# An encoder trunk on one core: the bias of group D in a query tile, the latents of group A through DRAM as one part

## The chip, the core and the metric

The kernel runs on one core of a Trainium2 chip. Such a core has five engines that run their own instruction streams in order: TensorE (PE, with its weight loads shown as PEld), VectorE (DVE), ScalarE (ACT), GpSimd (POOL) and SyncE (SP), which here issues nearly all transfers between DRAM and the on-chip memory SBUF. Matrix products land in PSUM, eight banks of 128 x 512 float32. The metric is the device time in microseconds of one execution. Three runs of the kernel before took 2723.59 to 2733.64 us, with a median of 2730.46.

## The reference

Two layers over 1024 tokens of width 1024, all in float32. Each layer: RMSNorm, one input projection, four groups of attention heads side by side, one output projection, then an MLP with squared ReLU. The groups, cut to what matters here:

```python
cq, ckv, kr, bq, bk, bv, ck.., dq, dk, dv = split(rms_norm(x, norm1_g) @ w_in)
# A (4 heads): queries, keys and values come from two small "latents"
q = rms_norm(cq, q_norm_g) @ w_uq          # cq: 192 wide, q_norm_g a gain per column
c = rms_norm(ckv, kv_norm_g)               # ckv: 128 wide
k, v = c @ w_uk, c @ w_uv
# B: differential attention, normed per head; dense like A
# C: each block of 128 queries sees 3 blocks of keys, with a mask
# D: neighbourhood on a 64-wide grid: scores + relative-position bias, softmax, values
mix = concat([rms_norm(y_a, g_a), y_b, rms_norm(y_c, g_c), rms_norm(y_d, g_d)])
x = x + mix @ w_out
```

## The kernel before

Every float32 product is made of three passes: operands are split into a high part (ACT copies it to the PE's format) and a low part (the rest, by DVE or POOL), and a product adds high x high, low x high and high x low (`passes`, L220 to L222). Operands lie transposed, columns on the 128 partitions, in tiles of 128 x 1024 or 128 x 512.

A layer's attention is woven from two streams (`weave`): one "main" stream of attention steps and one "fill" stream of projections. In order: the fused projections of B, then B's attention (`attn_b`) with the latents' projections (`proj_latent`) and D's projections as fill; then D's attention (`attn_d`) with C's projections and the latents' way up to A's queries, keys and values (`latent_up`) as fill; then C (`attn_c`) and A (`attn_a`) with the first half of the output projection as fill. A scheduler turns this into one fixed order of instructions for each engine, by priorities and by when buffers come free; only the MLP's PE order is written out by hand. Loads and stores all go to SP's queue in that order; the scheduler gives eight completion counters to them in turn, so that a transfer is not issued before the eighth before it has landed.

What the change and the prediction touch:

- Projected queries, keys and values are written to DRAM as two parts (`emit_parts`, `to_parts`, `to_values`) and loaded per head into tiles of the pool `xp` with the tag "x" (`stack`, eight of them for all groups): four per head in B and A, three per head in D (`qs`, two `ks`), four per pair of heads in C.
- The latents: `proj_latent` makes `cq` (128 + 64 rows) and `ckv` (128). `latent_parts` squares them for the norm, splits them with their gain into the two parts `both` (ACT L197, DVE L198) and stores these in `lat`, shape 2 x 3 x 128 x 1024. `latent_up` loads both parts into six tiles `latp` of the pool `big` (the 64-row one twice, into both halves of the partitions) and multiplies them (L220 to L222, and L720 for the 64-row one).
- `attn_d` loads a bias of 128 x 6 x 128 per head into one buffer "bias"; the mask of `attn_c` is loaded into the same buffer after it.
- `banded` makes a head of C or D: `score` (L977, then DVE's minimum with the bias or mask, L1053 or L1084, then the exponential on ACT), `parts` (transposes L986 and their split), `apply` (value sums, L998 and L999). The value sums of keys 0 to 4 go to the first half of the queries, then those of keys 3 to 7 to the second half. Each half starts with a matmul of zeros (`zeroed`, L1027) into the one bank "pv"; `pv_out` reads it out (ACT L746, DVE L188). PSUM is shared out as mm=2, tr=2, sb=3, pv=1; "mm" takes the products of the fill stream and small sums and transposes.
- `rstd_cols` sums squares over the partitions and makes reciprocal roots; `rows_of` turns its columns into rows in DRAM (`drows`), and `spread` loads such rows over the partitions (`rz`, `rq`, `rkv`). `sub_norm`, the norm of B per head, has two sums per column (g=2).

Of the kernel before, what the change touches and what calls it, by code (L numbers as in the profile page):

```python
# [13 lines left out]
F = mybir.dt.float32  # L14
R = mybir.dt.float32r
# [5 lines left out]
P = 128  # L21
S = 1024
# [6 lines left out]
T_CQ, T_CQR, T_CKV = 0, 1, 2  # L29
# [69 lines left out]
def layout(i):  # L99

    def padded(a, axis):

        z = np.zeros([1 if n == axis else s for n, s in enumerate(a.shape)], a.dtype)
        return np.concatenate([a, z], axis)

    n = LAYERS
    out = host_constants()
    out["x"] = i["x"][0].T.reshape(8, P, S)
    out["w_in"] = tiles_of(padded(i["w_in"], 2)[:, :, np.concatenate(input_tiles())], 4)

    wo = i["w_out"].reshape(n, 8, P, DM)[:, [2, 3, 6, 7, 4, 5, 0, 1]].reshape(n, DM, DM)
    out["w_out"] = tiles_of(wo, 4)
    out["w_up"] = tiles_of(i["w_up"], 4)
    out["w_down"] = tiles_of(i["w_down"], 4)

    uq = i["mla_w_uq"].reshape(n, 192, 4, 96)
    cols = [uq[..., 64:96].reshape(n, 192, 4, 2, 16).transpose(0, 1, 3, 2, 4).reshape(n, 192, P)]
    cols += [uq[:, :, 2 * t:2 * t + 2, 0:64].reshape(n, 192, P) for t in range(2)]
    q = np.stack(cols, 1)

    q = np.concatenate([q, q[:, :, 128:192]], 2).reshape(n, 6, P, P)
    kv = [i[w][:, None, :, t * P:(t + 1) * P] for w in ("mla_w_uk", "mla_w_uv") for t in range(2)]
    w = np.concatenate([q] + kv + [np.zeros((n, 2, P, P), uq.dtype)], 1)
    out["w_lat"] = w.reshape(n, 3, 4, P, P).transpose(0, 1, 3, 2, 4)
    rpb = padded(i["na_rpb"].reshape(n, 4, 465), 2)
    rpb[..., 465] = NEG
    out["bias"] = rpb[..., neighbours()]
    col = lambda a: a.reshape(n, -1, P).transpose(2, 0, 1).reshape(P, -1)
    gq = np.concatenate([i["mla_q_norm_g"], np.zeros((n, 64), np.float32)], 1)
    sub = np.concatenate([i["diff_subln_g"]] * 2, 1)  # L130
    lam = np.stack([i["diff_lambda_" + s] for s in ("q1", "q2", "k1", "k2")], 1)
    wide = lambda a: np.broadcast_to(a.reshape(1, -1), (P, a.size))
    out["par"] = np.concatenate(
        [col(i["norm1_g"]), col(i["norm2_g"]), i["final_norm_g"].reshape(8, P).T]
        + [col(i["out_g_" + s]) for s in ("mla", "swa", "na")]
        + [col(i["mla_kv_norm_g"]), col(gq), col(sub), wide(i["swa_sinks"])], 1)
    out["lam"] = wide(lam)
    return {k: np.ascontiguousarray(v) for k, v in out.items()}
# [7 lines left out]
class Trunk:  # L146
# [107 lines left out]
    def rstd_cols(self, sq, count, rhs, tag="mm"):  # L254

        nc = self.nc
        g = rhs.shape[1]
        n = sq.shape[1] // P
        ps = self.bank(tag, [P, n * g])
        for t in range(n):  # L260
            nc.tensor.matmul(ps[:, t * g:(t + 1) * g], sq[:, t * P:(t + 1) * P], rhs, start=True, stop=True)
        ms = self.cp.tile([P, n * g], F, tag="ms", name="ms")
        nc.vector.tensor_scalar(ms, ps, 1.0 / count, EPS, ALU.mult, ALU.add)
        return self.rsqrt_cols(ms)
# [15 lines left out]

    def spread(self, dst, rows, j=0, g=1):

        src = rows.rearrange("(t g) p -> g t p", g=g)[j]
        n = dst.shape[0]
        self.load(dst.rearrange("p (t q) -> p t q", t=8), src.partition_broadcast(n))

    def spread_here(self, dst, col):

# [88 lines left out]
    def attention(self, l):  # L377
        nc, tc, d = self.nc, self.tc, self.d
        rb = self.rb
        sbuf = lambda name, side="left": tc.tile_pool(name=f"{name}{l}", bufs=1, reuse_waits="tile", side=side)  # L380
        w_in = lambda t: d["w_in"][l, t]
        dr = lambda shape, name: self.dram.tile(shape, F, tag=name, bufs=1, name=name)
# [3 lines left out]
        qb, kb, vb = dr([2, 2, 4, 16, 2, S], "qb"), dr([2, 2, 4, 16, 2, S], "kb"), dr([4, P, 8, P], "vb")  # L386
        qd, kd, vd = dr([2, 2, P, S], "qd"), dr([2, 2, P, S], "kd"), dr([4, P, 8, P], "vd")
        qc, kc, vc = dr([2, 2, 2, 32, 2, S], "qc"), dr([2, 2, 32, 2, S], "kc"), dr([2, P, 8, P], "vc")
        lat, krd = dr([2, 3, P, S], "lat"), dr([2, 16, 2, S], "krd")
        qa = dr([2, 2, P, S], "qan"), dr([2, 4, 16, 2, S], "qar")  # L390
        ka, va = dr([2, 2, P, S], "kan"), dr([4, P, 8, P], "va")

# [25 lines left out]
        rows = []  # L418
        y = {"b": [], "d": [], "c": [], "a": []}
        with ExitStack() as stack, ExitStack() as att:  # L420
            self.ap = att.enter_context(sbuf("att"))
            with self.banks(mm=2, tr=2, sb=3, pv=1):
                with sbuf("proj", "right") as self.pp:
# [8 lines left out]
                    xs = self.normed(self.g1[:, l], lambda n: self.big_tile(R, n))  # L432
# [57 lines left out]
            with self.banks(mm=8):  # L490
# [12 lines left out]
                for m in range(self.EARLY, 8):  # L503
# [4 lines left out]
                    for n in range(2):  # L508
# [3 lines left out]
                        ps = self.mm_ps()  # L512
# [131 lines left out]
            self.keep(dst[:, :, n * 4:n * 4 + 4].rearrange("h p k e -> p h (k e)"), b.bitcast(F))  # L644
        return then

    def latent_parts(self, y, g, rows, n, dst, squares):

        nc = self.nc
        sl = slice(n * 512, n * 512 + 512)  # L650
        sq = self.part()
        nc.scalar.activation(sq[:rows], y[:rows], AF.Square)
        ps = self.bank("mm", [P, 4])
        for t in range(4):
            nc.tensor.matmul(ps[:, t:t + 1], sq[:rows, t * P:(t + 1) * P], self.ones[:rows, 0:1],
                             start=True, stop=True)
        nc.vector.tensor_copy(squares[:, n * 4:n * 4 + 4], ps)
        self.emit_parts(y[:rows], [(dst[:, :rows, sl].rearrange("a p s -> p a s"), slice(0, rows))],
                        slice(0, rows), g[:rows])

    def proj_latent(self, l, one, xs, rb, tabs, lat, krd, rows_out):


        nc = self.nc
        squares = [self.col("sq%d" % i, 8) for i in range(3)]
        for i, t, g in ((0, T_CQ, self.gq[:, l, 0:1]), (2, T_CKV, self.gkv[:, l:l + 1])):
            yield from one(t, xs, self.ev_plain(rb, lambda n, y: self.latent_parts(y, g, P, n, lat[:, i], squares[i])))
        c, s = tabs

        def ev(n, ps):  # L670
            sl = slice(n * 512, n * 512 + 512)
            y, t2 = self.part(), self.part()
            self.tt(y[0:64], ps[0:64], rb[0:64, sl])
            self.tt(y[64:112], ps[64:112], c[64:112, sl])
            self.tt(t2[64:80], ps[96:112], s[96:112, sl])
            self.tt(t2[96:112], ps[64:80], s[64:80, sl])
            self.tt(y[64:80], y[64:80], t2[64:80], ALU.add, self.eng)
            self.tt(y[96:112], y[96:112], t2[96:112], ALU.subtract, self.eng)
            self.emit_parts(y[64:112], [
                (krd[:, :, h, sl].rearrange("a p s -> p a s"), slice(64 + 32 * h, 80 + 32 * h))  # L680
                for h in range(2)], slice(64, 112))
            self.latent_parts(y, self.gq[:, l, 1:2], 64, n, lat[:, 1], squares[1])

        yield from one(T_CQR, xs, ev)
        q, k = squares[0], squares[2]
        self.tt(q, q, squares[1], ALU.add)
        for m, count in ((q, 192), (k, 128)):
            nc.vector.tensor_scalar(m, m, 1.0 / count, EPS, ALU.mult, ALU.add)
            rows_out.append(self.rows_of(self.rsqrt_cols(m)))
        yield True  # L690

    def latent_up(self, l, lat, rows, qa, ka, va):
# [2 lines left out]
        self.spread(rq, rows[0])  # L695
        self.spread(rkv, rows[1])
        parts = []
        for i, r in ((0, P), (1, 64), (2, P)):
            p = []
            for j in range(2):  # L700
                t = self.big_tile(R, "latp")
                for at in range(0, P, r):
                    self.load(t.bitcast(F)[at:at + r], lat[j, i, :r])
                p.append(t)
            parts.append(tuple(p))
        tabs = self.table("32", rq, nc.gpsimd)
        (qn, qr), kn = qa, ka

# [252 lines left out]
    def banded(self, qs, ks, v, y, j, finish, grid=False):  # L961
# [44 lines left out]
        for kb in range(8):  # L1006
            if kb + self.ahead < 8:
                score(kb + self.ahead)
            part = parts(kb)
            if kb in (3, 4):  # L1010
                held.append(part)
            if kb <= 4:
                apply(pv, 0, kb, part)
            else:
                apply(pv, 1, kb, part)
            if kb == 4:
                self.pv_out(pv, y, j, 0, grid)
                pv = self.zeroed()
                for i, p in enumerate(held):
                    apply(pv, 1, 3 + i, p)  # L1020
            yield True
        self.pv_out(pv, y, j, 1, grid)

    def zeroed(self):

        pv = self.bank("pv")
        self.nc.tensor.matmul(pv, self.zero, self.zero[:, 0:1].broadcast_to([P, 512]), start=True, stop=False)  # L1027
        return pv

    def attn_d(self, l, qd, kd, vd, ys):  # L1030
        nc = self.nc
        for t in range(2):
            y, rz = self.ypair(), self.rz_tile()
            for h2 in range(2):
                h = 2 * t + h2
                bias = self.ap.tile([P, 6, P], F, tag="bias", bufs=1, name="bias")
                self.load(bias, self.d["bias"][l, h])
                qs, ks = self.stack(), [self.stack() for _ in range(2)]
                rows = slice(h2 * 64, (h2 + 1) * 64)
# [22 lines left out]

    def attn_c(self, l, qc, kc, vc, ys):
        nc = self.nc
        mask = self.ap.tile([P, 6, P], F, tag="bias", bufs=1, name="mask")[:, 0:3]
        self.load(mask, self.d["swa"])
        for kv in range(2):
            ks = [self.stack() for _ in range(2)]
            for n, k in enumerate(ks):
# [421 lines left out]
```

## Time and profile before

| | |
|---|---|
| median of three runs | 2730.46 us |
| the profiled execution | 2728.97 us |
| its span, first to last instruction | 2727.2 us |
| PE busy | 2553.1 us, 94% |
| PE weight loads busy | 2110.1 us, 77% |
| DVE busy | 1994.1 us, 73% |
| ACT busy | 1430.9 us, 52% |
| POOL busy | 1134.5 us, 42% |
| moved by DMA | 389.20 MB, 143 GB/s on the mean |

The profile has the busy time of each engine, a table of slices or stretches with the granted share of the PE's clock and the DMA engines' busy share, groups of like instructions with the idle time before them and what ended it, the transfers, and a chain of waits that is followed back from the last instruction. L188 is the line of a helper, so that its groups are told apart by the tiles they write and read. A name such as `latp<-lat` means: written tile, read tile. Layer 0's attention runs to about 640 us, its MLP to about 1340 us; layer 1's attention begins at about 1400 us and its MLP at about 2000 us.

### The profile page before, as it was taken

What the parts mean: (1) busy time and instruction counts of PE and PEld (TensorE: products, weight loads), DVE (VectorE), ACT (ScalarE), POOL (GpSimd) and SP (SyncE); (2) the same over time, 40 slices, a digit from 0 to 9 for tenths busy, and PEclk for the clock granted to TensorE, in tenths of its full rate; (3) what the DMA queues carried; (4) which work ended last, traced back from release to release, by engine and by line L of the source; (5) the groups of instructions that cost most, each with busy time, mean ns of one, the idle gap of its engine ahead of it and who ended that gap; (6) DMA issues with size and microseconds to landing.
All of it is one profiled execution on the core that took longest, in us unless ns stands there. A gap on an engine that the chain in (4) does not pass through costs nothing.

```text
span 2727.2 us, 37613 instructions
## 1 busy us (share of the span) xinstructions
PE 2553.1 (94%) x12298; PEld 2110.1 (77%) x12298; DVE 1994.1 (73%) x3544; ACT 1430.9 (52%) x2547; POOL 1134.5 (42%) x754
## 2 busy tenths in 40 slices
PE   8989988899989999999999899889998999999997
PEld 6778876787778887888877688767886788878886
DVE  7787767674966669787567778677749666687786
ACT  4667757563534444444436676576635344444444
POOL 2555642111245554445435556331013455545552
PEclk9989999999989999999998899899999999999998
DMA  5534597231234447444244345972221444664431
GB/s 175 166 105 126 154 280 241 83 93 40 65 130 156 151 160 267 156 138 142 98 133 138 95 134 157 300 215 71 76 70 44 154 159 149 223 222 150 131 100 62
DMA packets 190516, 389.20 MB, mean 143 GB/s; under 512 B 23712, under 2 KB 30832, under 8 KB 190320
## 3 DMA queue, kind: packets, MB, share of 16 engines
q1 hardware_dynamic: 176496, 361.62, 43.0%
q10 hardware_dynamic: 13824, 25.17, 2.7%
q8 instruction: 98, 1.61, 0.3%
q14 instruction: 98, 0.80, 0.1%
HBM read 263.29 MB, written 123.41 MB: 142 GB/s over the span
## 4 chain that ended last, share of the span: by engine, by line
PE 70%; DVE 14%; DMA 7%; ACT 4%; issue 3%; SPq 1%; POOL 1%; DVEq 0%; ACTq 0%; POOLq 0%
PE u L220 8%; PE u L222 8%; PE u L221 8%; PE mm L220 5%; PE mm L221 5%; PE mm L222 5%; PE p L220 5%; PE p L221 5%; PE p L222 5%; PE sb L804 3%; PE tr L840 2%; DVE p L806 2%; DVE part L188 2%; PE pv L829 2%; PE pv L828 2%
## 5 line engine op out<-in xcount | busy, mean ns | idle before, releaser
L188 POOL TENSOR_TENSOR wl<-raw,wh 128x512 fp32r<-128x512 f32 x448 | 635.1, 1418 | 705.2 <-ACT wh L194 690.1
L194 ACT ACTIVATE wh<-raw 128x512 fp32r<-128x512 f32 x448 | 281.5, 629 | 579.8 <-PE u L221 315.0
L188 POOL TENSOR_TENSOR wl<-ws,wh 128x512 fp32r<-128x512 f32 (+1 forms) x112 | 148.1, 1325 | 456.9 <-ACT wh L194 426.0
L220 PE MATMUL u<-far,wh 128*128 128x512 f32 x768 | 301.5, 393 | 11.5 <-ACT ev L1237 8.3
L188 DVE TENSOR_TENSOR raw<-raw 128x512 f32<-128x512 f32 x256 | 226.4, 890 | 107.4 <-POOL wl L188 56.9
L222 PE MATMUL u<-far,wl 128*128 128x512 f32 x768 | 300.5, 391 | 1.9 <-POOL wl L188 1.9
L221 PE MATMUL u<-far,wh 128*128 128x512 f32 x768 | 300.3, 391 | 0.0
L188 DVE TENSOR_TENSOR ptl<-tr,pth 128x512 fp32r<-128x512 f32 (+2 forms) x384 | 238.3, 628 | 66.6 <-ACT pth L194 64.9
L809 ACT ACTIVATE p<-p,nm 128x1024 f32<-128x1024 f32 x192 | 220.1, 1147 | 99.8 <-DVE nm L806 98.9
L194 ACT ACTIVATE pth<-tr 128x512 fp32r<-128x512 f32 (+2 forms) x384 | 205.6, 546 | 121.0 <-PE tr L840 64.8
L220 PE MATMUL p<-far,wh 128*128 128x512 f32 x640 | 251.7, 393 | 7.6 <-DVE ev L188 7.6
L222 PE MATMUL p<-far,wl 128*128 128x512 f32 x640 | 250.9, 392 | 1.5 <-POOL wl L188 1.5
L221 PE MATMUL p<-far,wh 128*128 128x512 f32 x640 | 251.0, 392 | 0.0
L804 PE MATMUL sb<-stack 96*128 96x512 f32 x640 | 218.5, 424 | 24.7 <-DVE nm L806 24.0
L188 DVE TENSOR_TENSOR far<-act,far 128x512 fp32r<-128x512 f32 x224 | 208.6, 960 | 14.6 <-ACT far L194 14.6
L188 POOL TENSOR_TENSOR p<-p 128x1024 f32<-128x1024 f32 x64 | 154.3, 2415 | 141.1 <-ACT p L893 125.0
L220 PEld LDWEIGHTS u<-far,wh 128*128 128x128 f32 x768 | 145.4, 189 | 43.6 <-ACT ev L1237 9.2
L222 PEld LDWEIGHTS u<-far,wl 128*128 128x128 f32 x768 | 145.0, 189 | 33.2 <-POOL wl L188 2.7
L220 PE MATMUL mm<-xh,wh 128*128 128x512 f32 x416 | 169.4, 407 | 0.8 <-DVE rows L272 0.2
L806 DVE CUSTOM_DVE_ANT_0 p<-sb,zero,nm 128x512 f32<-128x512 f32 x192 | 142.4, 743 | 36.3 <-PE sb L804 32.8
L221 PEld LDWEIGHTS u<-far,wh 128*128 128x128 f32 x768 | 145.3, 189 | 30.2
L221 PE MATMUL mm<-xl,wh 128*128 128x512 f32 x416 | 166.6, 400 | 0.0
(243 smaller groups left out, 6147.0 us busy)
## 6 DMA issues: line engine op xcount, KB each, us to landing
act<-acts SPq DMA_DIRECT2D x224, 256.0 KB
raw<-in_w_up SPq DMA_DIRECT2D x128, 256.0 KB
acts<-ev SPq DMA_DIRECT2D x128, 256.0 KB
raw<-in_w_down SPq DMA_DIRECT2D x128, 256.0 KB
acts<-ev ACTq DMA_DIRECT2D x96, 256.0 KB
ws<-in_w_in SPq DMA_DIRECT2D x76, 256.0 KB
rz<-drows SPq DMA_DIRECT2D x40, 256.0 KB
stack<-kd SPq DMA_DIRECT2D x32, 256.0 KB
```

Source lines behind the costliest of these rows:

```text
L188: (eng or self.nc.vector).tensor_tensor(out=out, in0=a, in1=b, op=op)
L194: nc.scalar.activation(hi, src, AF.Copy)
L220: mm(ps, w[0], x[0][:, sl], start=start, stop=False)
L221: mm(ps, w[0], x[1][:, sl], start=False, stop=False)
L222: mm(ps, w[1], x[0][:, sl], start=False, stop=stop)
L804: self.nc.tensor.matmul(ps, q[:, qt * P:(qt + 1) * P], k[:, sl], start=i == 0, stop=i == len(passes) - 1)
L806: self.nc.vector.tensor_tensor_reduce(out=p[:, sl], in0=ps, in1=self.zero[:, 0:1].bitcast(F).broadcast_to([P, 512]), scale=-scale, scalar= ...
L809: self.nc.scalar.activation(p, p, AF.Exp, bias=nm[:, 1:2], scale=-1.0, accum_out=z)
L828: nc.tensor.matmul(out, v[:, kt], h[:, sl], start=kt == 0, stop=False)
L829: nc.tensor.matmul(out, v[:, kt], lo[:, sl], start=False, stop=kt == 7)
L840: nc.tensor.transpose(t[:, k * 256 + i * P:k * 256 + (i + 1) * P], p[:, (j * 2 + k) * P:(j * 2 + k + 1) * P], self.ident)
```

## The change

- The bias of a head of D is loaded into a tile of the pool of queries and keys (`stack`); a head of D so takes four of these tiles.
- C's mask gets a buffer of its own, whose load stands at the start of `attn_d`.
- The second half of a head's value sums in C and D goes to a bank "mm".
- The latents are stored as they come, in float32, and loaded into one tile each; the split with the gain is made there, in halves of 512 columns. The 64-row latent fills all 128 partitions, so its gain is repeated instead of being padded with zeros.
- `rstd_cols` orders its columns by group first, so that `spread` reads one run of 1024 numbers for each group.

```diff
-    gq = np.concatenate([i["mla_q_norm_g"], np.zeros((n, 64), np.float32)], 1)
+    gq = np.concatenate([i["mla_q_norm_g"], i["mla_q_norm_g"][:, 128:192]], 1)
...
-            nc.tensor.matmul(ps[:, t * g:(t + 1) * g], sq[:, t * P:(t + 1) * P], rhs, start=True, stop=True)
+            nc.tensor.matmul(ps.rearrange("p (g t) -> p t g", g=g)[:, t], sq[:, t * P:(t + 1) * P], rhs,
+                             start=True, stop=True)
...
     def spread(self, dst, rows, j=0, g=1):
-        src = rows.rearrange("(t g) p -> g t p", g=g)[j]
-        n = dst.shape[0]
-        self.load(dst.rearrange("p (t q) -> p t q", t=8), src.partition_broadcast(n))
+        src = rows.rearrange("(g t) p -> g (t p)", g=g)[j]
+        self.load(dst, src.partition_broadcast(dst.shape[0]))
...
-        lat, krd = dr([2, 3, P, S], "lat"), dr([2, 16, 2, S], "krd")
+        lat, krd = dr([3, P, S], "lat"), dr([2, 16, 2, S], "krd")
...
-    def latent_parts(self, y, g, rows, n, dst, squares):
+    def latent(self, y, rows, n, dst, squares):
         nc = self.nc
-        sl = slice(n * 512, n * 512 + 512)
+        self.keep(dst[:rows, n * 512:n * 512 + 512], y[:rows])
         sq = self.part()
...
         nc.vector.tensor_copy(squares[:, n * 4:n * 4 + 4], ps)
-        self.emit_parts(y[:rows], [(dst[:, :rows, sl].rearrange("a p s -> p a s"), slice(0, rows))],
-                        slice(0, rows), g[:rows])
...
-        for i, r in ((0, P), (1, 64), (2, P)):
-            p = []
-            for j in range(2):
-                t = self.big_tile(R, "latp")
-                for at in range(0, P, r):
-                    self.load(t.bitcast(F)[at:at + r], lat[j, i, :r])
-                p.append(t)
-            parts.append(tuple(p))
+        for i, (r, g) in enumerate(((P, self.gq[:, l, 0:1]), (64, self.gq[:, l, 1:2]), (P, self.gkv[:, l:l + 1]))):
+            t = self.big_tile(F, "latent")
+            for at in range(0, P, r):
+                self.load(t[at:at + r], lat[i, :r])
+            h, lo = self.big_tile(R, "lath"), self.big_tile(R, "latl")
+            for sl in self.halves():
+                self.split(h[:, sl], lo[:, sl], t[:, sl], g)
+            parts.append((h, lo))
...
                 self.pv_out(pv, y, j, 0, grid)
-                pv = self.zeroed()
+                pv = self.zeroed("mm")
...
-    def zeroed(self):
-        pv = self.bank("pv")
+    def zeroed(self, tag="pv"):
+        pv = self.bank(tag)
...
     def attn_d(self, l, qd, kd, vd, ys):
         nc = self.nc
+        self.mask = self.ap.tile([P, 3, P], F, tag="mask", bufs=1, name="mask")
+        self.load(self.mask, self.d["swa"])
...
-                bias = self.ap.tile([P, 6, P], F, tag="bias", bufs=1, name="bias")
+                bias = self.stack(F)[:, 0:6 * P].rearrange("p (a b) -> p a b", a=6)
                 self.load(bias, self.d["bias"][l, h])
...
     def attn_c(self, l, qc, kc, vc, ys):
         nc = self.nc
-        mask = self.ap.tile([P, 6, P], F, tag="bias", bufs=1, name="mask")[:, 0:3]
-        self.load(mask, self.d["swa"])
+        mask = self.mask
```

More of the change, by code (lines that the diff above doesn't have):

```diff
@@ L665, in proj_latent @@
         squares = [self.col("sq%d" % i, 8) for i in range(3)]
-        for i, t, g in ((0, T_CQ, self.gq[:, l, 0:1]), (2, T_CKV, self.gkv[:, l:l + 1])):
-            yield from one(t, xs, self.ev_plain(rb, lambda n, y: self.latent_parts(y, g, P, n, lat[:, i], squares[i])))
+        for i, t in ((0, T_CQ), (2, T_CKV)):
+            yield from one(t, xs, self.ev_plain(rb, lambda n, y: self.latent(y, P, n, lat[i], squares[i])))
         c, s = tabs
@@ L681, in ev @@
                 for h in range(2)], slice(64, 112))
-            self.latent_parts(y, self.gq[:, l, 1:2], 64, n, lat[:, 1], squares[1])
+            self.latent(y, 64, n, lat[1], squares[1])
         yield from one(T_CQR, xs, ev)
```

## The prediction

> **What bounds the kernel now.** I read the busy table by stretches first, because the shares of the whole span mix stages with different limits. Columns: start:end and length in us, then busy us (and instruction count) of PE, PEld, DVE, ACT and POOL, the granted TensorE clock, the DMA engines' mean busy share, GB/s.
>
> ```profile
> 280.00:340.00 60.00, 59.71 (x328) 50.87 (x327) 48.16 (x126) 43.86 (x74) 39.31 (x25) 1.00 0.49 137
> 340.00:500.00 160.00, 129.61 (x677) 103.87 (x676) 107.68 (x281) 96.02 (x242) 50.70 (x32) 0.91 0.80 239
> 500.00:640.00 140.00, 133.37 (x834) 114.51 (x833) 106.86 (x241) 89.76 (x158) 14.11 (x9) 1.00 0.23 69
> 640.00:1340.00 700.00, 678.07 (x2959) 556.41 (x2959) 500.67 (x632) 300.04 (x514) 324.95 (x231) 0.99 0.43 139
> 1700.00:1860.00 160.00, 135.42 (x713) 111.74 (x713) 112.45 (x299) 100.28 (x247) 46.94 (x30) 0.91 0.78 232
> ```
>
> Outside groups D and C the PE is 95 to 100% busy and sets the time; nothing there is changed in amount. In D and C (340 to 500 and 1700 to 1860) it sits idle 30.4 and 24.6 us and is granted 0.91 of its clock, while the DMA engines are at 0.80. The table in steps of 20 us shows that the DMA is full in its first half:
>
> ```profile
> 340.00:360.00 20.00, 19.77 (x112) 16.93 (x111) 10.95 (x30) 11.46 (x32) 7.52 (x6) 1.00 1.01 274
> 360.00:380.00 20.00, 12.70 (x74) 10.54 (x73) 8.69 (x20) 9.30 (x21) 9.52 (x5) 1.00 1.03 296
> 400.00:420.00 20.00, 14.79 (x82) 12.13 (x81) 13.27 (x35) 12.70 (x32) 4.95 (x3) 0.91 1.02 296
> ```
>
> So here the PE waits for data, and the chain of waits (start us, us, what) names which:
>
> ```profile
> 365.69 11.75 DMA latp<-lat
> 396.36 1.89 SPq L160
> 399.02 5.40 DMA bias<-in_bias
> 404.43 9.07 DMA stack<-kc
> 413.57 9.20 DMA kan<-both
> ```
>
> The waits of the PE in the two stages (us in total, times, longest) say the same; the first five rows are of 340 to 500, the last three of 1700 to 1860:
>
> ```profile
> PE mm L720 <- DMA latp<-lat: 2.7, 2, 2.2
> PE mm L221 <- DMA latp<-lat: 2.4, 1, 2.4
> PE mm L220 <- DMA latp<-lat: 1.3, 1, 1.3
> PE pv L1027 <- DVE y L188: 3.2, 4, 1.5
> PE mm L220 <- DVE part L188: 1.1, 1, 1.1
> ...
> PE pv L1027 <- DVE y L188: 3.4, 4, 1.4
> PE mm L221 <- DMA latp<-lat: 2.8, 1, 2.8
> PE mm L720 <- DMA latp<-lat: 2.5, 2, 1.9
> ```
>
> **Latents as one part.** The DMA table (issues, KB each) gives what is moved now:
>
> ```profile
> lat<-both SPq DMA_DIRECT2D x8, 512.0 KB
> latp<-lat SPq DMA_DIRECT2D x8, 512.0 KB
> latp<-lat SPq DMA_DIRECT2D x8, 256.0 KB
> lat<-both SPq DMA_DIRECT2D x4, 256.0 KB
> ```
>
> Loads: 8 x 512 + 8 x 256 KB = 6.29 MB over both layers, and half of that, 3.15 MB, goes. The stage moves 239 GB/s at a share of 0.80, so about 299 GB/s when full: 10.5 us for both layers. The PE's own waits for these loads are 2.7 + 2.4 + 1.3 + 2.8 + 2.5 = 11.7 us, so the two readings agree; bounds 0 (something else fills the queue) and -11.7. The halved stores fall at 106 to 173 us, where the DMA isn't full: nothing, covered by PE work.
>
> The split into a high and a low part moves from ahead of the store to behind the load. Its rows in the first layer (ns min/median/max):
>
> ```profile
> L197 ACT ACTIVATE both<-part,par x6: 707/710/724, 103.3 to 165.3; 128x512 fp32r<-128x512 f32 x4, 64x512 fp32r<-64x512 f32 x2
> L198 DVE SCALAR_TENSOR_TENSOR both<-part,par,both x6: 732/744/2385, 104.1 to 172.1; 128x512 fp32r<-128x512 f32 x4, 64x512 fp32r<-64x512 f32 x2
> ```
>
> Twelve of each in both layers. Behind a load they stand on the path once per layer (0.71 + 0.74 us until the first half can be multiplied; the second half and the other latents follow while the PE works): +2.9 us. The rest, 12 x 0.74 = 8.9 us of DVE and 8.5 of ACT, meets engines 67% and 60% busy; I take +2, with bounds 0 and 8.9. What queues behind a split that waits for its load are the exponentials and evictions of group D on ACT and the score reductions on DVE, and the PE waits for those. Where the splits leave, DVE is full only once per layer:
>
> ```profile
> 160.00:170.00 10.00, 6.02 (x21) 4.28 (x20) 10.00 (x17) 5.95 (x9) 9.84 (x5) 0.67 0.34 119
> 1510.00:1520.00 10.00, 2.88 (x11) 1.95 (x9) 9.93 (x19) 4.15 (x7) 8.31 (x4) 0.51 0.20 74
> ```
>
> Two splits of each layer lie in or beside that stretch: 4 x 0.74 = -3.0 (0 if the reciprocal-root chain there only closes up). Latents together: -10.5 + 2.9 + 2 - 3 = -8.6.
>
> **Bias in a query tile.** There is one bias buffer now, so the load for the next head is issued after the last score of this one, and lands late in a full queue:
>
> ```profile
> 347.13 0.41 DVE L1053 CUSTOM_DVE_ANT_0 p<-sb,bias 128x256 f32<-128x256 f32 x1
> 347.57 0.34 SPq L160 DMA_DIRECT2D bias<-in_bias  x1
> 354.52 0.42 DVE L1053 CUSTOM_DVE_ANT_0 p<-sb,bias 128x256 f32<-128x256 f32 x1
> ...
> L1053 DVE CUSTOM_DVE_ANT_0 p<-sb,bias 128x256 f32<-128x256 f32 x16 | 6.7, 420 | 3.2 <-DMA bias<-in_bias 3.0
> ```
>
> Head 1's first score follows head 0's last by 7.4 us. In the built program of the changed kernel the bias load stands with the head's query and key loads, one head ahead, and the next head's scores directly behind the last. The price is depth: four of the eight tiles per head instead of three, so loads two heads ahead go. Direct waits are small (the last row: DVE waited 3.0 us in all for bias), but the first layer's chain has the 5.40 us: I take -5 for both layers, bounds 0 and -10.8. Mask in its own place: its load moves to the start of the kernel, hidden there; 0.
>
> **Second half's sums in a bank of the projections.** The group of zeroing matmuls (x count | busy us, mean ns | idle us before them):
>
> ```profile
> L1027 PE MATMUL pv<-zero 128*128 128x512 f32 x32 | 15.4, 480 | 8.0 <-DVE y L188 6.6 <-DVE yc L188 1.1
> L188 DVE TENSOR_TENSOR part<-mm,tabc 128x512 f32<-128x512 f32 x16 | 11.0, 688 | 6.5 <-PE mm L720 3.3 <-PE mm L222 3.1
> L188 DVE TENSOR_TENSOR part<-mm,tabs 64x512 f32<-64x512 f32 x32 | 22.0, 688 | 0.5
> ```
>
> At most the 8.0 us go. But only two banks "mm" exist. The scheduler has put the first head's zeroing matmul long before its use, four projection products ahead, so these share one bank: each must be read out (0.69 + 2 x 0.69 = 2.1 us, the two lower rows) before the next may start, 8.3 us per layer if nothing stands between. In the new order 18 to 22 other PE instructions do, so I take half a microsecond to one each, +6 for both layers; bounds 0 and 16.6. Sum -2, bounds -8.0 and +8.6.
>
> **The spread of B's norm** is now one run per row instead of eight pieces; compare the issue on SP:
>
> ```profile
> 396.36 2.57 SPq L160 DMA_DIRECT2D rz<-drows  x2
> 483.24 0.90 SPq L160 DMA_DIRECT2D rz<-drows  x2
> ```
>
> 1.7 us per pair, one pair per layer inside the full stretch and on the chain at 396.36: -2, bounds 0 and -3.4. Bytes stay.
>
> **Sum**: -8.6 - 5 - 2 - 2 = -17.6 us. The profiled execution took 2728.97 (span 2727.2 and 1.8 around it), so 2711.4; the median of the runs is 1.5 higher, so I say 2713.
>
> One rule of the Trainium skill would make the sum larger. The rows of 160 and 1510 us above have PE idle 4.0 and 7.1 of 10 us and a granted clock of 0.67 and 0.51. "TensorE: Matmul & The Clock Gate", section "What's actually happening", says in my words that an idle window of about 3.4 us drops the array to half clock until it has been busy for as long again; those rows agree. By it each long gap that closes pays up to 1.7 us more, an estimate from that page, so four of them would make it 2706; the sum goes without.
>
> **Rivals.** (1) Slower: the held bank decides. If every product next to a held bank waits for its eviction, the four above (8.3) and one at each of the other seven heads (14.5), that is 22.8 us per layer, 45.6 in all, in place of the +6; the rest of the sum is -23.6, so +22: 2752. For it: the PE works in order, and only 1.1 us per layer of such waits stand there with two free banks. Against: heads 1 to 3 and C have short products, and their banks are held a few us only. It decides from about 12 us per layer.
> (2) No change: what is freed is taken by the next transfer of the chain, kc (9.07) and kan (9.20), which stay. Then only the bank's -2 and the -3 where DVE was full remain, about 2726. For it: the share of 1.02 at 400 to 420.
> (3) The splits meet POOL. In the row above one took 2385 ns, at 104.08, while POOL ran from 103.51 to 108.73. If all twelve did, 12 x 1.64 = 19.7 us more, all on the path: 2733.
>
> ```profile
> 104.08 2.38 DVE L198 SCALAR_TENSOR_TENSOR both<-part,par,both 128x512 fp32r<-128x512 f32 x1 [1.23 <-ACT both L197]
> 103.51 5.22 POOL L188 TENSOR_TENSOR p<-p 128x1024 f32<-128x1024 f32 x2 [6.89 <-ACT p L893]
> ```
>
> Against: the median of the six was 744. The page "SBUF — State Buffer", section "Who interferes with whom", says that a DVE instruction with two SBUF inputs is blocked by a GpSimd one that reads SBUF; the row agrees, and the moved splits keep two SBUF inputs.
> (4) More: bias, latents and bank together let the PE run through. Half of the 55.0 idle us and the clock from 0.91 to 0.95 (265 busy us x 4%, 11) make -38: 2692.
>
> **How the numbers follow.** Forecast 0.42, its own range 2703 to 2723; rival 1 0.23, rival 2 0.15, rival 3 0.06, rival 4 0.14. 0.5%, 13.7 us, is about what a measurement of this kernel can tell. Faster: 0.36 of the forecast and all of (4), 0.50. Slower: (1) and a little of the others, 0.26. Same: 0.24. The range takes in (4) at 2690 and stops short of the end of (1), at 2746.
>
> **What would show it.** Right: PE idle in the two D and C stretches down by 15 to 20 us, no wait "DMA bias" left, the waits for the latents (now on ACT) under 3 us per layer, DMA share full for some 5 us less per layer. Wrong: waits of "mm" products for DVE over 12 us per layer (rival 1); the same idle time with kc, qc or va in the chain (2); splits of over 2 us (3). Any change in the stretch 640 to 1340, whose instructions keep their order, would be wrong for all of them.

## The result and the profile after

The changed kernel takes 2746.43 us in the median of four runs (2744.3 to 2747.79), against 2731.2 us for the kernel before beside it: a ratio of 1.006, 95% interval 1.0039 to 1.0081. It is slower by some 15 us, where 2713 was forecast. Its profiled execution took 2747.79 us, with a span of 2745.9.

In the kernel after, most of the lines spoken of stand two lower: L1027 (zeroing) is L1025, L977 and L986 are L975 and L984, L998 and L999 are L996 and L997, L746 is L744, L720 is L718. First the stretches again, with the columns of the prediction's first fence.

```profile
280.00:340.00 60.00, 57.08 (x305) 47.26 (x304) 48.10 (x113) 41.80 (x70) 38.82 (x23) 0.97 0.50 143
340.00:500.00 160.00, 125.82 (x668) 103.47 (x666) 105.18 (x282) 94.48 (x242) 45.03 (x30) 0.90 0.79 223
500.00:640.00 140.00, 131.59 (x800) 113.67 (x800) 106.80 (x241) 90.31 (x158) 21.07 (x12) 0.98 0.26 74
640.00:1340.00 700.00, 677.04 (x2975) 555.91 (x2973) 503.88 (x636) 302.61 (x518) 320.42 (x228) 0.99 0.43 139
1700.00:1860.00 160.00, 127.88 (x661) 103.63 (x660) 106.11 (x277) 94.66 (x239) 48.33 (x31) 0.89 0.79 226
```

The loss is in groups D and C: in the two stretches PE is idle 34.2 us in the first layer and 32.1 in the second, where it was 30.4 and 24.6. The scores of D and C, from the first start to the last, take 161.8 us in the first layer, as this row of after has them; before, they took 141.7 (its row stands further down):

```profile
L975 PE MATMUL sb<-stack x128: 275/338/668, 329.4 to 491.2; 128*128 128x384 f32 x96, 128*128 128x256 f32 x32
```

The MLP's stretch, 640 to 1340, is as it was (677.04 busy us against 678.07). The PE's waits (us in total, times, longest) name a new one; first those of 340 to 500, then those of 1700 to 1880:

```profile
PE mm L1025 <- DVE both L188: 9.4, 1, 9.4
PE mm L996 <- ACT pth L194: 7.6, 3, 5.1
...
PE mm L1025 <- DVE part L188: 1.5, 1, 1.5
...
PE mm L220 <- ACT lath L197: 0.7, 1, 0.7
...
PE mm L221 <- DVE latl L198: 0.4, 1, 0.4
```

```profile
PE mm L1025 <- DVE both L188: 8.5, 1, 8.5
...
PE mm L220 <- ACT lath L197: 1.4, 1, 1.4
PE mm L221 <- DVE latl L198: 0.7, 1, 0.7
```

The waits for latents are small now, and none for the bias is left, as forecast. In their place a zeroing product of a second half waits 9.4 us in one layer and 8.5 in the other, for a bank `mm` that the last step of another read-out (the transposed values, into `both`) frees. The chain of waits has two stores in the full DMA queue just there, which hold the two buffers `both`:

```profile
415.81 5.81 DMA qan<-both
421.71 0.64 ACT both L194
422.42 1.27 POOL both L188
423.71 9.34 DMA kan<-both
```

The second of these is still under way when the wait ends. What the read-out in question waited for is the store of `kan` before it, issued at 419.53. The timeline has that store, ScalarE's half of the read-out, and the zeroing product itself (start us, us, what, and in brackets the idle time before it):

```profile
419.53 0.53 SPq L167 DMA_DIRECT2D kan<-both  x1
427.87 0.60 ACT L642 ACTIVATE both<-mm 128x512 fp32r<-128x512 f32 x1 [0.89 <-DMA kan<-both]
429.34 0.77 PE L1025 MATMUL mm<-zero 128*128 128x512 f32 x1 [9.44 <-DVE both L188]
```

That was the first theory of the cause. It points at the right bank, but, as the runs below show, at the wrong hold of it.

### The profile page after: what moved, and what is told of

It reads as the page before. It is cut to its first block, busy times and chain, and to the rows that moved or that the text cites. A ratio compares the mean times of both kernels' runs of the same rounds, so it can differ in the third digit from the quotient of the medians.

```text
span 2745.9 us, 37645 instructions
## 1 busy us (share of the span) xinstructions
PE 2560.8 (93%) x12298; PEld 2115.5 (77%) x12298; DVE 1979.5 (72%) x3544; ACT 1429.6 (52%) x2547; POOL 1133.0 (41%) x754
## 2 busy tenths in 40 slices
DMA packets 184755, 383.43 MB, mean 140 GB/s; under 512 B 23584, under 2 KB 26608, under 8 KB 184560
## 4 chain that ended last, share of the span: by engine, by line
PE 72%; DVE 14%; DMA 5%; ACT 4%; issue 3%; POOL 1%; SPq 0%; DVEq 0%; ACTq 0%; POOLq 0%
PE u L220 8%; PE u L222 8%; PE u L221 8%; PE mm L220 5%; PE mm L221 5%; PE p L220 5%; PE p L221 5%; PE p L222 5%; PE mm L222 5%; PE sb L802 3%; DVE p L804 2%; PE tr L838 2%; DMA rz<-drows 2%; DVE part L188 2%; DVE ptl L188 2%
## 5 line engine op out<-in xcount | busy, mean ns | idle before, releaser
L838 PE MATMUL tr<-ident,p 128*128 128x128 f32 x1024 | 160.7, 277 | 7.8 <-DVE ptl L188 6.9
```

What stands on the lines that cost most here:

```text
L838: nc.tensor.transpose(t[:, k * 256 + i * P:k * 256 + (i + 1) * P], p[:, (j * 2 + k) * P:(j * 2 + k + 1) * P], self.ident)
```

## Experiments

Every kernel was timed beside the kernel before: after in four executions, the others in 5 to 12. "Of before" is the ratio to it, with its 95% interval.

| kernel | what differs | median us | of before |
|---|---|---|---|
| after | the whole change | 2746.43 | 1.0060 (1.0039 to 1.0081) |
| mm_alone | before, second half in `mm` | 2745.74 | 1.0063 (1.0049 to 1.0077) |
| bias_alone | before, bias and mask | 2720.69 | 0.9978 (0.9967 to 0.9988) |
| latents_alone | before, latents | 2720.92 | 0.9980 (0.9971 to 0.9988) |
| spread_alone | before, spread | 2723.93 | 0.9995 (0.9982 to 1.0007) |
| no_spread | before, bias, mask and latents | 2722.91 | 0.9992 (0.9980 to 1.0004) |
| pv_back | after, second half in `pv` | 2725.48 | 0.9993 (0.9984 to 1.0002) |
| both3 | after, three buffers `both` | 2744.18 | 1.0061 (1.0047 to 1.0076) |
| pv_back_both3 | both of the last two | 2708.54 | 0.9928 (0.9909 to 0.9948) |
| sb_bank | after, second half in `sb` | 2706.90 | 0.9922 (0.9907 to 0.9938) |
| tr_bank | after, second half in `tr` | 2746.86 | 1.0075 (1.0059 to 1.0092) |
| tr_bank_both3 | the same, three buffers `both` | 2739.34 | 1.0048 (1.0033 to 1.0064) |
| mm3_sb2 | after, three banks `mm`, two `sb` | 2742.91 | 1.0057 (1.0042 to 1.0073) |
| sb2_control | the same, second half in `pv` | 2752.95 | 1.0091 (1.0074 to 1.0108) |
| sb_alone | before, second half in `sb` | 2711.15 | 0.9939 (0.9926 to 0.9952) |
| sb_bank_both3 | sb_bank, three buffers `both` | 2703.54 | 0.9916 (0.9902 to 0.9931) |
| first_pv | after, only each layer's first head in `pv` | 2720.80 | 0.9975 (0.9965 to 0.9985) |
| first_mm | after, only each layer's first head in `mm` | 2738.11 | 1.0044 (1.0027 to 1.0062) |

### One part at a time

pv_back takes the bank's part out of the change:

```diff
-                pv = self.zeroed("mm")
+                pv = self.zeroed()
```

> The changed kernel, with the second half's value sums back in the bank pv; the other parts stay. Theory A (the held bank: the second half's zeroing product waits for a bank mm, whose reader waits for a buffer both, whose store waits in the full DMA queue; 9.4 and 8.5 us at one place of each layer): these two waits go, some 4 us per layer for the sums of the half before come back, 2731 to 2720 us, most likely 2724. Theory B (depth: the bias takes one of eight tiles, so a head's loads can be issued only one head ahead, and they come late): 2741 to 2750. Theory C (the latents' splits queue behind their load on ScalarE and VectorE): 2741 to 2750 too.

The other three put one part into the kernel before: mm_alone the reverse of the line above, bias_alone and latents_alone the bias with the mask, and the latents, as the change has them.

> The kernel before, with nothing but the second half's value sums moved to a bank mm. Theory A: slower than before by 8 to 20 us, 2739 to 2751, with a wait of a zeroing product for the writer of both of 5 us or more in each layer. Theories B and C: 2724 to 2731, the waits for y (8.0 us) gone and nothing in their place.

> The kernel before, with nothing but the bias in a query tile and the mask in its own place. Theory B: slower than before, 2738 to 2748, the loads of heads 2 and 3 of group D landing later than before. Theories A and C: 2722 to 2731.

> The kernel before, with nothing but the latents through DRAM as one part (split behind the load). Theory C: slower than before, 2738 to 2748, with ScalarE or VectorE busy on the splits while PE waits for a score or a value product. Theories A and B: 2719 to 2728, 3.15 MB less moved in groups D and C and no wait of PE for the latents over 2 us.

Measured: 2725.48, 2745.74, 2720.69 and 2720.92. Theories B and C fall: bias and latents each gain 6 us. The bank alone costs 17 us (0.63% of 2726.5), the whole loss and a little more. But bias, latents and spread without the bank gain nothing that can be told from zero, although two of them gain alone. One sign of theory A is missing: in mm_alone the zeroing product waits for the writer of `both` for 6.1 us in the second layer, but for 3.4 in the first, less than the 5 asked for, and the loss is there in full.

### The buffers behind the bank, and the spread

```diff
-        return self.pp.tile([P, 2, 512], R, tag="both", bufs=2, name="both")
+        return self.pp.tile([P, 2, 512], R, tag="both", bufs=3, name="both")
```

> The changed kernel with three buffers both in place of two, and nothing else. Theory A1 (the held bank is late because the reader of the other bank mm waits for a buffer both that a store in the full DMA queue holds): the waits of the zeroing products for the writer of both, 9.4 and 8.5 us, fall under 4 us, 2728 to 2738 us, most likely 2733. Theory A2 (the reader is late by its place in the queues of ScalarE and VectorE, or the products themselves are late, and the buffer only happens to be there): the waits stay over 6 us, 2741 to 2749.

> The changed kernel with the second half's sums back in the bank pv, and with three buffers both. If the stores that hold both also set the pace where no bank is held (a wait of 4.7 us of a latent product for the writer of both, behind a store of va of 9.3 us, in the second layer of that kernel with two buffers): 2712 to 2721. If the full DMA queue is what counts, and a third buffer only lets more stores queue: 2722 to 2729.

> The kernel before with nothing but the new order of the norm's columns and the spread in one run per row. By the prediction's term: 2722 to 2727, the SyncE issue of a pair at 0.9 us in place of 2.6. If it eats the gain of the other two parts (bias alone and latents alone each gained 6 us, all three parts without the held bank only 1): slower than before, 2732 to 2738.

> The kernel before with bias, mask and latents changed, and neither the spread nor the bank of the second half. If the spread eats their gain, or the two gains add: 2713 to 2718. If bias and latents fill the same idle time: 2719 to 2727.

With three buffers the waits named above all but go; these are PE's in both3, in 340 to 500 and in 1700 to 1860:

```profile
PE mm L1025 <- DVE both L188: 2.5, 1, 2.5
...
PE mm L1025 <- DVE both L188: 2.1, 1, 2.1
```

Yet the time stays, 2744.18. Neither theory had that: A1 was right on the waits, A2 on the time. The longest wait in the trace was not the price of the held bank. With it all but gone PE is idle for 30.2 and 27.6 us in the two stretches, 8.5 us less than in after, and yet the first layer's last score of C begins at 497.3 us, not at 491.2. Without the held bank, the same third buffer is worth 0.65% (0.9928 against 0.9993), 18 us; at 2708.54 the kernel lies below the 2712 us expected at best. Most of this lies in the second layer, where the scores of D and C take 145.2 us in place of 167.4 (in the first, 145.7 in place of 149.7). So the two buffers `both` limit groups D and C once the bank does not. The spread alone is within the noise of zero, and without it bias and latents still gain only 2 us: it is these two that don't add.

### Which bank

In sb_bank and tr_bank the name of the bank changes; mm3_sb2 keeps `mm` and shares PSUM out anew:

```diff
-            with self.banks(mm=2, tr=2, sb=3, pv=1):
+            with self.banks(mm=3, tr=2, sb=2, pv=1):
...
-                        return [(self.bank(a), self.bank(b)) for a, b in (("sb", "sb"), ("sb", "tr"), ("tr", "pv"))]
+                        return [(self.bank(a), self.bank(b)) for a, b in (("sb", "sb"), ("mm", "tr"), ("tr", "pv"))]
```

> The changed kernel with the second half's sums in one of the three score banks sb; the projections keep both banks mm, two buffers both. Theory A3 (the price is that one of the two banks of the fill stream is held through half of each head, so that the latents' products are put a head later in the fixed order of TensorE and read out one at a time; waiting for a buffer both is only how it shows): the latents start in head 1 again and the time is that of the kernel with the sums in pv or a little less, 2718 to 2728 us. Theory A4 (any second bank held through half a head costs as much, wherever it is taken from, or the gain of a second bank for the sums is what misplaces the work): 2738 to 2750.

> The same with one of the two transposing banks tr. Theory A3: 2718 to 2732 us, the latents in head 1 again; the one bank left for transposes costs something (a transpose waits for the low part of the one before). Theory A4: 2740 to 2752.

> The changed kernel, second half in mm, but with three banks mm and two sb in place of two and three; the fused projections of B take an mm bank where they took the third sb. Theory A3: with two banks left to the fill stream the loss of about 19 us goes, less what the missing score bank costs, 2715 to 2732 us. Theory A4: 2740 to 2752, as the bank is held as before.

> The changed kernel with the second half in a bank tr and three buffers both. If the sums in a second bank are worth what the trace of before shows (8.0 us of waits for the one bank pv, here against the kernel with the sums in pv and three buffers both, 2708.5): 2698 to 2706 us. If what is left is the DMA, or the one transposing bank takes it back: 2706 to 2716.

sb_bank comes out at 2706.90, better than A3 had it and far from A4. tr_bank and mm3_sb2 miss A3 by 15 and 11 us and by their times fit A4; tr_bank_both3 misses by 23. For mm3_sb2 the trace shows where. The scores of D and C, of before and then of mm3_sb2 (x count: ns min/median/max, first and last start):

```profile
L977 PE MATMUL sb<-stack x128: 274/338/667, 333.6 to 475.3; 128*128 128x384 f32 x96, 128*128 128x256 f32 x32
```

```profile
L975 PE MATMUL sb<-stack x128: 274/338/686, 361.2 to 501.9; 128*128 128x384 f32 x96, 128*128 128x256 f32 x32
```

D begins 27.6 us later, after group B with one score bank less; from there D and C take 140.7 us against 141.7. The bank taken away from B hides what is asked, so a control was needed:

> The same banks as in the kernel with three mm and two sb, but the second half's sums in the one bank pv. Theory A3 (a bank held in mm costs where it leaves the fill stream one, and not where it leaves two): no faster than that kernel by more than 6 us, 2737 to 2750 us; what both lose against before is the missing score bank in group B. Theory A4 (any held bank of the fill stream costs the 19 us): 2718 to 2730.

It takes 2752.95, 3 us above A3's range: with two banks `mm` left, the held one costs nothing but gains 0.34% (1.0057 against 1.0091), 9 us. A4 falls. And the bank is held there for longer than in after, 98.2 us by the first head of the first layer, from its zeroing product to its read-out:

```profile
315.58 0.38 PE L1025 MATMUL mm<-zero 128*128 128x512 f32 x1
...
413.79 0.60 ACT L744 ACTIVATE pvt<-mm 64x512 f32<-64x512 f32 x1
```

tr_bank loses in another way. None of its holds of a bank `tr` is over 23.1 us, and the latents begin at 369.6 us in the first layer, not much behind the 367.0 of before, as A3 had it. So it is not the late fill; whether it is slow for the one transposing bank that it leaves was not taken apart.

> The kernel before with nothing but the second half's sums in a score bank sb. If a second bank for the sums is worth its waits (8.0 us for the one bank pv): 2717 to 2725. If it is worth as much as beside the other parts of the change (18 us between the sums in pv and in sb): 2705 to 2714. If the score bank's loss eats it: 2725 to 2735.

> The changed kernel with the second half in a bank sb and three buffers both. If the two gains (sums in sb instead of pv 18 us, third buffer both 17 us) add: 2688 to 2696. If they close the same idle time of TensorE: 2698 to 2708.

sb_alone gains 0.61%, 17 us, by nothing but one word against mm_alone, which loses 17. It holds a score bank for 14 to 38 us in every head, the first and the seven others alike. Its zeroing products hardly wait any more for the read-out of the half before (`y` or `yc`). These rows of the group, weight loads included, say what they waited for, in all (us, times); in before the same view has 15.8 us for `y` and 5.4 for `yc`:

```profile
its engine sat idle before it (us, times) until:
  DVE nb L1084: 1.2, 2
  DVE yc L188: 0.7, 2
  DVE nb L1053: 0.6, 2
  PE sb L977: 0.4, 1
```

sb_bank_both3 is the fastest, 2703.54, but not to be told from sb_bank. The gains of `sb` and of the third buffer don't add either; that they close the same idle time, as the expectation has it, fits the time and was not looked into further.

### One long hold or seven short ones

What is bad about `mm` is seen in the timeline of after from the first head's zeroing product to its read-out. The rows between are DVE's, taking C's last projections out of `mm`:

```profile
321.72 0.38 PE L1025 MATMUL mm<-zero 128*128 128x512 f32 x1
...
325.21 0.69 DVE L188 TENSOR_TENSOR part<-mm,tabc 128x512 f32<-128x512 f32 x1
...
340.42 0.69 DVE L188 TENSOR_TENSOR part<-mm,tabc 128x512 f32<-128x512 f32 x1 [0.54 <-PE mm L222]
...
351.60 0.68 DVE L188 TENSOR_TENSOR part<-mm,tabc 128x512 f32<-128x512 f32 x1
...
364.10 0.68 DVE L188 TENSOR_TENSOR part<-mm,rb 128x512 f32<-128x512 f32 x1
...
381.67 0.60 ACT L744 ACTIVATE pvt<-mm 64x512 f32<-64x512 f32 x1
...
383.37 0.67 DVE L188 TENSOR_TENSOR part<-mm,rb 128x512 f32<-128x512 f32 x1
```

In the kernel before the same five products are read out at these times:

```profile
325.60 0.69 DVE L188 TENSOR_TENSOR part<-mm,tabc 128x512 f32<-128x512 f32 x1
...
333.97 0.69 DVE L188 TENSOR_TENSOR part<-mm,tabc 128x512 f32<-128x512 f32 x1
...
344.30 0.69 DVE L188 TENSOR_TENSOR part<-mm,tabc 128x512 f32<-128x512 f32 x1 [0.48 <-PE mm L222]
...
355.82 0.69 DVE L188 TENSOR_TENSOR part<-mm,rb 128x512 f32<-128x512 f32 x1
...
363.86 0.69 DVE L188 TENSOR_TENSOR part<-mm,rb 128x512 f32<-128x512 f32 x1
```

The bank is held for 60.0 us, from before the head's first score, and the four products after the first take 58.2 us in place of 38.3. In the second layer the hold is 53.6 us. The holds of the other heads are between 3.6 and 19.8 us. Two kernels take the first head's hold and the seven others apart. first_pv has the first head's sums in `pv`:

```diff
-                pv = self.zeroed("mm")
+                first, self.seen = not getattr(self, "seen", 0) % 8, getattr(self, "seen", 0) + 1
+                pv = self.zeroed("pv" if first else "mm")
```

first_mm has the two names exchanged.

> The changed kernel, with the second half of each layer's first head (head 0 of D) in pv, and the second halves of the other seven heads in mm as in the changed kernel. Theory H (the scheduler issues the first head's zeroing product as soon as a bank mm is free, and the bank is held 60.0 us in the first layer and 53.6 in the second, in which the last projections of C share one bank): the loss of 18 us goes, 2717 to 2732. Theory S (the short holds of 1 to 20 us of the other heads cost it): 2739 to 2750.

> The counterpart: only the first head's second half in mm, the other seven in pv. Theory H: as slow as the changed kernel, 2738 to 2750. Theory S: as the kernel with all sums in pv, 2720 to 2731.

first_pv takes 2720.80, 0.25% less than before; first_mm 2738.11, 0.44% more. Theory H holds, and S falls: seven of eight holds are harmless or help (one of them lasts 30.6 us in first_pv), and one in each layer turns the gain into a loss. The start of the latents, read from the first of their products in the first layer, goes along with it; the rows are of before, after, first_pv and first_mm, one fence each:

```profile
L220 PE MATMUL mm<-latp,wh x14: 387/476/775, 367.0 to 437.7; 128*128 128x512 f32 x14
```

```profile
L220 PE MATMUL mm<-lath,wh x14: 390/465/775, 385.6 to 447.3; 128*128 128x512 f32 x14
```

```profile
L220 PE MATMUL mm<-lath,wh x14: 393/489/775, 370.2 to 438.2; 128*128 128x512 f32 x14
```

```profile
L220 PE MATMUL mm<-lath,wh x14: 393/478/792, 386.7 to 442.9; 128*128 128x512 f32 x14
```

While the bank is held PE is no more idle than before, as two stretches of after show: it is 87% busy until 382, with D's heads, and 76% from there to 500. In the kernel before the same two have 87 and 81%, in pv_back 88 and 86%.

```profile
321.00:382.00 61.00, 53.22 (x289) 45.23 (x288) 34.58 (x94) 35.85 (x85) 23.56 (x15) 0.94 0.78 207
382.00:500.00 118.00, 89.58 (x467) 72.14 (x465) 83.43 (x222) 71.43 (x180) 33.47 (x21) 0.88 0.79 227
```

So in after the price is paid behind the hold: the projections that should fill PE's gaps come 19 us late, D's heads run ahead of them, and the latents' way up, with its stores, is pushed into C. This reading of how the late fill becomes lost time fits both3 too, where the latents begin at 385.9. It is argued and not shown, and the size doesn't follow from it. In mm_alone the latents come 19.4 us late in the first layer (386.4 against 367.0), but the first product of that layer's MLP out of `far` comes only 2.9 us later than in before; from there to the same product of the second layer it loses another 13.3. After against pv_back has 19.6 and 4.3 us, first_mm against pv_back 15.2 and -2.8. These are single executions, so a few us are noise; still, the price of one hold is not told by its length. What is shown is that the holds of the two first heads together make the loss: against pv_back first_mm still loses 14 of the 18 us, and without these two holds first_pv loses nothing.

## Why the prediction was wrong

**What bounds the kernel.** Right in the main: the loss lies in groups D and C, and 640 to 1340 did not change. "95 to 100% busy" outside them was too much: in before PE has 65.23 of the first 75 us, 60.02 of the 70 from 150 and 60.68 of the 70 from 1510. That PE waits for data there was half of it: the data that it waits for come through two banks `mm` and two buffers `both`, and the page of the profile shows such a limit only as a wait for whatever frees them.

**Latents, -8.6.** Right in sign; alone they are worth 0.20% or 5.5 us (3.3 to 7.9 by the interval). PE's waits for them fell from 11.7 to 3.2 us (0.7 + 0.4 and 1.4 + 0.7 in the second layer, for both parts), by about what was said. ScalarE waited 3.6 us for their loads in the first layer and 4.3 in the second, a little over the 3 given. The bytes went (389.20 MB in all, now 383.43), but the DMA engines' share in the two stretches did not fall: 0.79 in both, where it was 0.80 and 0.78. The gain from the stretch where DVE is full is there, too. These rows, 150 to 190 us, are of before, after and latents_alone:

```profile
150.00:190.00 40.00, 30.02 (x138) 23.74 (x137) 34.58 (x88) 24.54 (x38) 22.82 (x12) 0.79 0.29 80
```

```profile
150.00:190.00 40.00, 32.85 (x146) 25.29 (x145) 30.06 (x88) 24.17 (x38) 25.10 (x15) 0.83 0.27 77
```

```profile
150.00:190.00 40.00, 32.23 (x150) 24.74 (x149) 30.88 (x89) 24.75 (x39) 26.28 (x15) 0.83 0.26 77
```

DVE has 4.5 us less to do there, and PE is busy 2.8 us longer, with the latents alone 2.2; 1.5 per layer were said, and the size depends on the ends chosen, as from 160 to 180 it is 0.9. Some of the splits did meet POOL, as rival 3 had it: two of the twelve took 2.04 and 2.02 us, three more 1.7 to 1.8, where the median is 0.75, and POOL was at work beside each. First the first of them, with POOL's work beside it, then all twelve:

```profile
384.71 2.38 POOL L188 TENSOR_TENSOR tabs<-tabs,rq 128x1024 f32<-128x1024 f32 x1
385.61 2.04 DVE L198 SCALAR_TENSOR_TENSOR latl<-latent,par,lath 128x512 fp32r<-128x512 f32 x1
```

```profile
L198 DVE SCALAR_TENSOR_TENSOR latl<-latent,par,lath x12: 735/751/2039, 385.6 to 1755.5; 128x512 fp32r<-128x512 f32 x12
```

That is 5.7 us of DVE in all, not 19.7, and PE waited for `latl` for 1.1 us only.

**Bias, -5, and mask, 0.** Right: together 6.0 us (3.3 to 9.0).

**Spread, -2.** Not told from zero: 1.4 us, between 4.9 gained and 1.9 lost. The issue of the pair in the full stretch did get shorter:

```profile
416.96 1.33 SPq L160 DMA_DIRECT2D rz<-drows  x2
```

It was 2.57 there before.

**That the terms add.** This step failed. Bias and latents gain 6.0 and 5.5 alone but 2.2 together (no_spread). Each term was read from its own wait in the same stretch, and when one wait goes another takes its place. The third buffer `both`, which brings 18 us on top of pv_back, says that stores holding these buffers were next. Rival 2 had seen that kan's store stays, and left it there as an end, not as something to be moved. Why a wait of the one hides just behind that of the other was not taken apart, and whether a third buffer helps the kernel before wasn't tried.

**The bank, -2 with -8.0 and +8.6 as its ends.** This is the step that failed worst, and it turned the sign. It measured +17 alone and +18 with the rest (1.0060 against 0.9993). The place was right: the first head's zeroing product stands long before its use, and four projection products share one bank meanwhile. The size was not: half a microsecond to one was taken for each, and 2.1 us, the read-out, as the most. In after the four come 19.9 us later in the first layer, 5.0 each. A product that shares its bank does not only wait for the read-out; it is put behind the next pieces of the main stream in the fixed order, and the fill comes late as a whole. The upper end of the gain failed too: the 8.0 us of waits for `pv` were taken as the most that a second bank can bring, and in sb_alone it brings 17.

**Rivals.** Rival 1, "the held bank decides", came nearest, 2752 against 2746. But it laid two thirds of its price, 14.5 of 22.8 us per layer, on the seven other heads; first_pv shows that these cost nothing, so that its time was in part luck. Rival 2 was nearer than the sum for the rest of the change: without the bank it leaves -3 us and the sum -15.6, and pv_back has -1.9 (-4.4 to +0.5). Rival 4's way was open, with other means: sb_bank_both3, with another bank and one more buffer, has 2703.54, two thirds of the way from 2726.76 to its 2692.

## What to carry to other kernels

A second buffer for one stream is taken from another, and in these runs its price went with how many that one has left: from three score banks it gained 17 us, from two projection banks it lost 17, with all else in the source alike, and with a third projection bank a hold of 98 us did no harm. Before lending out one of two banks, look in the built order for where its first instruction stands, since a scheduler may open it as soon as one is free and hold it for 60 us; the lender's work then comes late as a whole, and not by one read-out. Short holds are no proof of safety: tr_bank, with none over 23 us, lost 20. The longest wait in a trace is a place to look and not a price: here one of 9 us could be taken away without a gain, until the thing behind it had gone.

## What the runs showed of the hardware

A store of 512 KB that only empties a buffer is felt when the DMA engines are full: in the chain above the stores of qan and kan stand with 5.81 and 9.34 us, and from 415 to 434 us the engines are at a share of 1.03. With two such buffers the writers wait for the stores; one buffer more, with no byte less moved (383.41 MB in both), took 18 us from the kernel (pv_back_both3 against pv_back).
